# Six blocks of an MLP's second product by Strassen's algorithm, on one core

## Chip, cores and metric

The kernel runs on one core of a Trainium2 chip. The metric is the device time of one execution in microseconds (us).

## What is computed

The reference is a trunk of two layers over 512 tokens of 1024 channels, in float32. Each layer is a token mixer and an MLP with a hidden width of 4096. A conditioning vector `c` gives each of the four sub-layers a shift, a scale and a gate (`ada_mod`, one product of `c` with a matrix of 1024 by 3072):

```python
m = (jax.nn.silu(c) @ w + b)[:, None, :]
shift, scale, gate = jnp.split(m, 3, axis=-1)
...
u = x * (1.0 + scale) + shift
y = jnp.square(jax.nn.relu(u @ mlp_w1[layer] + mlp_b1[layer])) @ mlp_w2[layer] + mlp_b2[layer]
x = layer_norm(ALPHA * x + (1.0 + gate) * y, ln_g[layer, 1], ln_b[layer, 1])
```

The change is in the second MLP (`mlp(1, ...)`, the last piece of the program), in its product with `mlp_w2`, and in where the gate of that MLP is worked out.

## The kernel before

Every large product is made of three matmuls: each float32 operand is split into a rounded high part and a low part, and high × high, high × low and low × high are added up in PSUM. ScalarE (ACT) writes the high part by a cast, VectorE (DVE) the low part by a subtraction. For weights the parts are `wh` and `wl`, made from a staged slab `ws` of 1 MB (two buffers); for the hidden activations they are `hh` and `hl`, made from `r`, the output of the ReLU.

An MLP (`mlp`, L1043) cuts its hidden width into 8 blocks of 512. `up(b)` (L1048) makes one block of hidden channels for all 512 tokens: 4 slices × 8 pieces of the depth × 3 = 96 matmuls of 128 x 512. `down(b)` (L1080) multiplies that block with 512 rows of `mlp_w2` and adds into `Y`, held as 4 token tiles × 2 halves of 512 columns: 4 × 2 × 4 × 3 = 96 matmuls. The order is up(0), then up(1), down(0), up(2), down(1), to down(7).

Weights come by a list, `self.wlist` (`plan_weights`, L311): `w_dma` (L356) loads the next slab on the queue of SyncE (SP), `w_pre` (L394) splits it, `w_take` hands it to the product. A load waits until the split of the slab two places earlier is done.

The shifts, scales and gates are made piece by piece while an MLP runs. `ada_steps` (L209) is a generator: one step loads two tiles `ast` of a matrix, scales them and adds them into `acc`; four steps finish one job of 512 columns; after that two `pada` matmuls with a matrix of ones sum `acc` over its partitions (`finish`, L232). One of two generators does its additions on POOL (GpSimd), with the scaling on ACT, the other on DVE. `tick()` (L290) moves both by one step. The loops of `up` and `down` call it twice each, so 28 times in the first MLP; `self.tick(99)` behind the loop, ahead of down(7), runs what is left. The first MLP's list has six jobs (L1508). The gate of the last MLP, the jobs (3, 4) and (3, 5), is started in the last MLP:

```python
            if b == 1 and last:
                self.ada = [self.ada_steps([(3, 4)], "g", True), self.ada_steps([(3, 5)], "v", True)]
```

When a job is done and another follows, `acc` is split into `acch` and `accl`, and its sum is two matmuls of 512 columns; the last job's sum is one fp32 matmul.

In the last MLP POOL also works on the residual rows (`residuals`, L559, called by `step`): 16 additions or products of 128 x 512 (`X`) and 4 scalings (`rA`, `rB`).

Calls to the engines go through a helper, so the profile gives nearly all of them line L50; tiles are told apart by name. A scheduler fixes each engine's order when the program is built, and each engine and each DMA queue works its list in order.

Of the kernel before, what the change touches and what calls it, by code (L numbers as in the profile page):

```python
# [18 lines left out]
P = 128  # L19
# [17 lines left out]
PRED = mybir.dt.uint32  # L37

# [35 lines left out]
class Trunk:  # L74
# [26 lines left out]
    def setup(self):  # L101
# [29 lines left out]
        self.gate_d = {2: self.dram.tile([1, D], F32, name="gated2")}  # L131
# [77 lines left out]
    def ada_steps(self, jobs, eng, halved):  # L209
# [22 lines left out]
        def finish(n, cb, *acc):  # L232
            pt = self.ps("pada")
            for q, a in enumerate(acc):
                nc.tensor.matmul(pt, self.ones if len(acc) == 1 else self.ones_r, a,
                                 start=(q == 0), stop=(q == len(acc) - 1))
            if cb < 4:
                row = self.s2(f"mrow{n}_{cb}")[0:1, :]
                nc.scalar.copy(row, pt[0:1, :])
                nc.sync.dma_start(self.mod_d[n][:, cb * 512:cb * 512 + 512], row)  # L240
            else:
                h = cb - 4
                if n == 2:
# [7 lines left out]
                if n == 2:  # L251
                    nc.sync.dma_start(self.gate_d[n][:, h * 512:h * 512 + 512], g)
# [58 lines left out]
    def plan_weights(self):  # L311
# [5 lines left out]

        def out(w, n):
# [4 lines left out]
        def mlp(l):  # L323
            w1, w2 = i["mlp_w1"][l], i["mlp_w2"][l]
            up = lambda b: [("ch", w1, b * 512, 256), ("ch", w1, b * 512 + 256, 256)]
            dn = lambda b: [("rows", w2, b * 512, 2 * l + 1), ("rows", w2, b * 512 + 256, 2 * l + 1)]
            L.extend(up(0))
# [3 lines left out]

        self.wsmall = set()

        def alternate(n0):
            for q in range(n0, len(L)):
                if (q - n0) // 2 % 2:
                    self.wsmall.add(q)

        n0 = len(L)
        out(i["ev_w_out"][0], 0)  # L340
        mlp(0)
        alternate(n0)
# [7 lines left out]
        out(i["od_w_out"][0], 2)  # L350
        mlp(1)
        alternate(n0)
# [3 lines left out]
    def w_dma(self):  # L356
        d = self.wlist[self.n_dma]
        kind, w = d[0], d[1]
        if kind == "ch":
# [34 lines left out]
    def w_pre(self, eng=None):  # L394
# [8 lines left out]
        kind = d[0]  # L403
        small = self.n_split in self.wsmall
# [18 lines left out]
        self.n_split += 1  # L423

# [618 lines left out]
    def mlp(self, l, X, rest, last):  # L1043
# [4 lines left out]
        def up(b):  # L1048
            hh, hl = self.u8("hh"), self.u8("hl")
            ws = self.w_take() + self.w_take()  # L1050
# [10 lines left out]
            for f in range(4):  # L1061
                if b == 0:
# [3 lines left out]
                if f % 2 == 0:  # L1066
                    self.w_pre()
                col = 64 + l * 32 + b * 4 + f
                r, h2 = self.s2("r"), self.s2("h2")
# [8 lines left out]
            return hh, hl  # L1078

# [424 lines left out]
    def run(self):  # L1504
# [3 lines left out]
        self.ada = [self.ada_steps([(1, 4), (2, 0), (2, 2), (2, 4), (3, 0), (3, 2)], "g", True),  # L1508
                    self.ada_steps([(1, 5), (2, 1), (2, 3), (2, 5), (3, 1), (3, 3)], "v", True)]
# [32 lines left out]
```

## Time and profile before

| | |
|---|---|
| runs | 1270.35, 1271.13, 1271.96 us |
| median | 1271.13 us |
| profiled execution | 1276.4 us, of which the span is 1274.7 us |
| mean granted clock of TensorE | 0.988 of full speed |
| busy share of PE, DVE, ACT, POOL | 96%, 72%, 46%, 40% |
| read from HBM | 172.1 MB |

The profile is of one execution, with times from the start of its span. PE is TensorE's matmul side, PEld its weight loads, SPq the queue of loads and stores. A row of the timeline groups equal instructions in a row; a bracket at its end gives the idle time before it and what ended it. Matmuls overlap at their ends, so their pitch is read from their starts. In the profile the first MLP ends at about 600 us; the last one begins at 911 and runs to the end.

### The profile page before, as it was taken

To read this page: it belongs to the slowest core of one execution; us is meant where nothing else is said; L and a number is where in the kernel's file an instruction comes from. 1 tells how busy PE (TensorE), PEld (TensorE's weight loads), DVE (VectorE), ACT (ScalarE), POOL (GpSimd) and SP (SyncE) were. 2 spreads that over 40 slices of the span, in tenths; PEclk is the share of its full clock that TensorE was granted. 3 is DMA by queue.
4 is the path that set the end of the run, shared out by engine and by line. 5 is a ranking of instruction groups with operands and counts; after the bars stand their busy time and mean duration, and the time that the engine had idled before them with its cause. 6 is when DMAs were issued, how large, how long until landed. Compare 5 with 4: busy or idle time off the path is not lost. (4 is left out here: it accounts for less than half of the span.)

```text
span 1274.7 us, 17852 instructions
## 1 busy us (share of the span) xinstructions
PE 1226.4 (96%) x6529; PEld 1044.1 (82%) x6529; DVE 917.2 (72%) x1470; ACT 587.0 (46%) x1028; POOL 513.3 (40%) x524
## 2 busy tenths in 40 slices
PE   5899899999999999999999999999899999999997
PEld 4687678888888888888999999887888788888886
DVE  7879887867878766879578878778767745543656
ACT  2376553453544443523666677752453332322321
POOL 3466421538312320376256557558438000000166
PEclk9899999999999999999999999999899999999999
DMA  9757414262775456524232232343261624232311
GB/s 282 213 198 262 169 63 157 96 225 74 248 255 195 162 198 231 178 87 118 83 101 84 67 93 67 109 165 100 83 232 67 214 66 132 71 114 81 133 33 66
DMA packets 131529, 177.51 MB, mean 139 GB/s; under 512 B 9270, under 2 KB 87764, under 8 KB 131442
## 3 DMA queue, kind: packets, MB, share of 16 engines
q1 hardware_dynamic: 131330, 176.33, 43.0%
q8 instruction: 51, 0.84, 0.3%
q14 instruction: 36, 0.29, 0.1%
q10 hardware_dynamic: 112, 0.05, 0.0%
HBM read 172.10 MB, written 4.26 MB: 138 GB/s over the span
## 5 line engine op out<-in xcount | busy, mean ns | idle before, releaser
L50 DVE TENSOR_TENSOR wl<-ws,wh 128x512 fp32r<-128x512 f32 (+1 forms) x255 | 269.8, 1083 | 69.4 <-ACT wh L50 64.7
L50 ACT CAST wh<-ws 128x1024 fp32r<-128x1024 f32 (+2 forms) x271 | 207.7, 808 | 202.1 <-PE p L50 81.4
L50 PE MATMUL p<-uh,wh 128*128 128x512 f32 (+1 forms) x576 | 206.2, 366 | 0.0
L50 PE MATMUL p<-uh,wl 128*128 128x512 f32 (+1 forms) x576 | 205.9, 365 | 0.0
L50 PE MATMUL p<-wh,hh 128*128 128x512 f32 (+1 forms) x516 | 201.0, 390 | 0.0
L50 PE MATMUL p<-wh,hl 128*128 128x512 f32 (+1 forms) x516 | 200.0, 388 | 0.0
L50 PE MATMUL p<-wl,hh 128*128 128x512 f32 (+1 forms) x516 | 199.9, 387 | 0.0
L50 PE MATMUL p<-ul,wh 128*128 128x512 f32 (+1 forms) x576 | 192.9, 366 | 0.0
L50 POOL TENSOR_TENSOR acc<-acc,ast 128x512 f32<-128x512 f32 x70 | 102.8, 1468 | 205.1 <-ACT ast L50 111.7
L50 DVE TENSOR_TENSOR h<-r 128x512 f32<-128x512 f32 x64 | 52.7, 826 | 125.9 <-ACT r L50 124.6
L50 PEld LDWEIGHTS p<-uh,wl 128*128 128x128 f32 x576 | 108.7, 189 | 17.6
L50 PEld LDWEIGHTS p<-uh,wh 128*128 128x128 f32 x576 | 108.6, 189 | 17.4
L50 PEld LDWEIGHTS p<-ul,wh 128*128 128x128 f32 x576 | 100.9, 189 | 17.3
L50 PEld LDWEIGHTS p<-wl,hh 128*128 128x128 f32 x516 | 96.9, 188 | 20.2 <-issue 0.5
L50 PEld LDWEIGHTS p<-wh,hh 128*128 128x128 f32 x516 | 96.9, 188 | 20.0 <-ACT hh L50 0.2
L50 PEld LDWEIGHTS p<-wh,hl 128*128 128x128 f32 x516 | 96.9, 188 | 19.9
L50 ACT ACTIVATE r<-p,colA 128x512 f32<-128x512 f32 x64 | 43.8, 685 | 148.4 <-PE p L50 148.1
L50 POOL TENSOR_TENSOR ws<-ws,gate 128x512 f32<-128x512 f32 x16 | 25.0, 1596 | 210.9 <-DMA ws<-in_mlp_w_dram 210.9
L50 DVE TENSOR_TENSOR Y<-Y,p 128x512 f32<-128x512 f32 x96 | 64.7, 680 | 41.0 <-PE p L50 40.3
L50 DVE SCALAR_TENSOR_TENSOR acc<-ast,cs,acc 128x512 f32<-128x512 f32 x70 | 83.8, 1198 | 14.2 <-DMA ast<-in_ada_w_dram 13.8
L50 ACT ACTIVATE ast<-ast,cs 128x512 f32<-128x512 f32 x70 | 49.8, 721 | 93.2 <-DMA ast<-in_ada_w_dram 91.1
L50 POOL TENSOR_TENSOR ul<-u,uh 128x512 fp32r<-128x512 f32 x32 | 44.5, 1403 | 82.8 <-ACT uh L50 70.0
(317 smaller groups left out, 2686.2 us busy)
## 6 DMA issues: line engine op xcount, KB each, us to landing
ws<-in_mlp_w_dram SPq DMA_DIRECT2D x64, 1024.0 KB
ast<-in_ada_w_dram SPq DMA_DIRECT2D x160, 256.0 KB
ws<-in_od_w_in_dram SPq DMA_DIRECT2D x16, 1024.0 KB
ast<-in_ada_w_dram SPq DMA_DIRECT2D x16, 512.0 KB
ws<-in_ev_w_in_dram SPq DMA_DIRECT2D x7, 1024.0 KB
ws<-in_ev_w_out_dram SPq DMA_DIRECT2D x4, 1024.0 KB
nf<-fd SPq DMA_DIRECT2D x16, 256.0 KB
ws<-in_od_w_out_dram SPq DMA_DIRECT2D x4, 1024.0 KB
```

What stands on the lines that cost most here:

```text
L50: x = f(*a, **k)
```

## The change

The last MLP works in three groups of two hidden blocks, then two blocks as before. In a group, `up(g, True)` and `up(g + 1, True)` keep the hidden block unsplit (`hr`, float32). The product of 512 tokens × 1024 hidden × 1024 columns is then taken as a 2 × 2 product of blocks of 256 tokens × 512 hidden and 512 hidden × 512 columns, in Winograd's form of Strassen's algorithm: seven block products, each of 2 × 4 × 3 = 24 matmuls. `factor` forms the sums of hidden blocks (S1 to S4) in place in `hr` and splits them into high and low parts (`ha`, or `hah` and `hal`); `wino_b` does the same for the weights (T1 to T4, in `ws` and in four tiles `wE`), which `wino_dma` loads; B22 is loaded twice. The results stay in PSUM where two products share a sum, or go to `U2`, `Q7`, `Q5`, `C11`, `D21`, `D12` in SBUF, which are put together after the third group.

The gate of the last MLP moves: its jobs (3, 4) and (3, 5) are the seventh of the first MLP's lists, and its row goes through DRAM (`gated`, like that of the sub-layer before) and is read back ahead of up(6).

```diff
+WINOGRAD = (1,)
+WINO_B = ("B11", "T3", "T1", "T2", "B21", "T4", "B22")
+WINO_A = ("A11", "S3", "S1", "S2", "A12", "A22", "S4")
+WINO_SRC = {"B11": (0, 0), "T3": (0, 1), "B21": (1, 0), "B22": (1, 1)}
...
-                if n == 2:
+                if n >= 2:
                     g = self.s2(f"grow{n}_{h}")[0:1, :]
...
+            if l in WINOGRAD:
+                for g in range(0, 6, 2):
+                    L.extend(up(g) + up(g + 1) + [("wino", w2, g * 512, x) for x in WINO_B])
+                L.extend(up(6) + up(7) + dn(6) + dn(7))
+                for b in (n0 + 2, len(L) - 6, len(L) - 2):
+                    self.wsmall |= {b, b + 1}
+                return
...
+    def wino_dma(self, w, r0, which):
+        nc = self.nc
+        block = lambda r, c: w[r:r + 512, c:c + 512].rearrange("(k p) f -> p k f", p=P)
+        st = None
+        if which in WINO_SRC:
+            r, c = WINO_SRC[which]
+            st = self.wp.tile([P, 4, 512], F32, tag="ws", bufs=WS_BUFS, name="ws")
+            nc.sync.dma_start(st, block(r0 + 512 * r, 512 * c))
+        if which == "T3":
+            E = [self.s2(f"wE{k}") for k in range(4)]
+            for k in range(4):
+                nc.sync.dma_start(E[k], w[r0 + 512 + k * P:r0 + 512 + k * P + P, 512:1024])
+            self.wE_next = E
+        self.wstage[self.n_dma] = st
+        self.n_dma += 1
+    def wino_b(self, which, st):
+        nc = self.nc
+        sub = lambda o, a, b: nc.vector.tensor_tensor(o, a, b, op=ALU.subtract)
+        r = []
+        def halves(src, a):
+            hi, lo = [self.wp.tile([P, 2, 512], F32R, tag=x, name=x) for x in ("wh", "wl")]
+            if isinstance(src, list):
+                for j in range(2):
+                    nc.scalar.copy(hi[:, j], src[a + j])
+                    sub(lo[:, j], src[a + j], hi[:, j].bitcast(F32))
+            else:
+                nc.scalar.copy(hi, src[:, a:a + 2, :])
+                sub(lo, src[:, a:a + 2, :], hi.bitcast(F32))
+            return [(hi[:, j], lo[:, j]) for j in range(2)]
+        if which == "B11":
+            self.wB11 = st
+        elif which == "T3":
+            self.wE, self.wB12 = self.wE_next, st
+            for k in range(4):
+                sub(self.wE[k], self.wE[k], st[:, k])
+        if which == "T1":
+            for a in (0, 2):
+                x = self.wB12[:, a:a + 2, :]
+                sub(x, x, self.wB11[:, a:a + 2, :])
+                r += halves(self.wB12, a)
+            for k in range(4):
+                nc.vector.tensor_tensor(self.wE[k], self.wE[k], self.wB11[:, k], op=ALU.add)
+            return r
+        for a in (0, 2):
+            r += halves(self.wE if which in ("T3", "T2", "T4") else st, a)
+        if which == "B21":
+            for k in range(4):
+                sub(self.wE[k], st[:, k], self.wE[k])
+        return r
...
-        def up(b):
+        def up(b, raw=False):
+            if raw:
+                hh, hl = self.u8("hr", F32), None
+            else:
+                hh, hl = self.u8("hh"), self.u8("hl")
+            ws = self.w_take() + (self.w_take() if b == 0 or not raw else [])
...
                 nc.scalar.activation(hh[:, f], r, AF.Square)
-                nc.vector.tensor_tensor(h2, r, r, op=ALU.mult)
-                nc.vector.tensor_tensor(hl[:, f], h2, hh[:, f].bitcast(F32), op=ALU.subtract)
+                if not raw:
+                    h2 = self.s2("h2")
+                    nc.vector.tensor_tensor(h2, r, r, op=ALU.mult)
+                    nc.vector.tensor_tensor(hl[:, f], h2, hh[:, f].bitcast(F32), op=ALU.subtract)
...
+        def factor(name, H, q):
+            a = [H[0][:, :, 0:256], H[0][:, :, 256:512]] + ([H[1][:, :, 0:256], H[1][:, :, 256:512]] if H[1] else [])
+            sub = lambda o, x, y: nc.vector.tensor_tensor(o, x, y, op=ALU.subtract)
+            if q % 3 < 2:
+                t = self.u8("ha", F32R, (2, 4, 256))
+                parts = [(slice(0, 4), t[:, 0], t[:, 1])]
+            else:
+                parts = [(slice(f, f + 2), *[self.s2(x, F32R).rearrange("p (k t) -> p k t", k=2) for x in ("hah", "hal")])
+                         for f in (0, 2)]
+            if name == "S3":
+                sub(a[1], a[0], a[1])
+            elif name == "S1":
+                sub(a[1], a[3], a[1])
+                nc.vector.tensor_tensor(a[0], a[0], a[1], op=ALU.add)
+            elif name == "S4":
+                sub(a[2], a[2], a[1])
+            src = a[{"A11": 0, "S3": 1, "S1": 0, "S2": 1, "A12": 2, "A22": 3, "S4": 2}[name]]
+            terms = []
+            for fs, hi, lo in parts:
+                nc.scalar.copy(hi, src[:, fs])
+                sub(lo, src[:, fs], hi.bitcast(F32))
+                terms += [(hi[:, k], lo[:, k]) for k in range(fs.stop - fs.start)]
+            return terms
+        def winograd(g, acc, H, first):
+            ops = list(first)
+            pts = {}
+            plan = [("1", False, "U2", None), ("7", False, "Q7", None), ("5", False, "Q5", 1), ("6", False, "U2", None),
+                    ("1", True, "C11", 0), ("7", True, "D21", 0), ("5", True, "D12", 1)]
+            for q, (bank, on, to, bias) in enumerate(plan):
+                if len(ops) < min(q + 3, 7):
+                    ops.append(factor(WINO_A[len(ops)], H, len(ops)))
+                w = self.w_take()
+                self.w_pre()
+                if not on:
+                    pts[bank] = [self.ps("p2") for _ in range(2)]
+                for k in range(4):
+                    for t in range(2):
+                        tok = slice(t * P, t * P + P)
+                        lh, ll = [x[:, tok] for x in ops[q][k]]
+                        for n3, (x, y) in enumerate(((lh, w[k][0]), (lh, w[k][1]), (ll, w[k][0]))):
+                            nc.tensor.matmul(pts[bank][t], x, y, start=(not on and k == 0 and n3 == 0),
+                                             stop=(k == 3 and n3 == 2), skip_group_check=True)
+                ops[q] = None
+                for t in range(2):
+                    if (to, t) in acc:
+                        nc.vector.tensor_tensor(acc[to, t], acc[to, t], pts[bank][t], op=ALU.add)
+                        continue
+                    acc[to, t] = self.s2(f"{to}{t}")
+                    if bias is None:
+                        nc.vector.tensor_copy(acc[to, t], pts[bank][t])
+                    else:
+                        nc.vector.tensor_tensor(acc[to, t], b2[bias], pts[bank][t], op=ALU.add)
...
-        Y = [[self.s2(f"Y{t}_{h}") for h in range(2)] for t in range(NT)]
-        prev = up(0)
-        for b in range(1, nb):
-            if b == 1 and last:
-                self.ada = [self.ada_steps([(3, 4)], "g", True), self.ada_steps([(3, 5)], "v", True)]
-            cur = up(b)
-            down(b - 1, *prev)
+        if l in WINOGRAD:
+            acc = {}
+            for g in range(0, 6, 2):
+                H = [up(g, True)[0], None]
+                first = [factor(WINO_A[q], H, q) for q in range(2)]
+                H[1] = up(g + 1, True)[0]
+                winograd(g, acc, H, first)
+            for t in range(2):
+                for x, y in (("D12", "U2"), ("D21", "U2"), ("Q7", "Q5"), ("Q7", "U2")):
+                    nc.vector.tensor_tensor(acc[x, t], acc[x, t], acc[y, t], op=ALU.add)
+            Y = [[acc["C11", t], acc["D12", t]] for t in range(2)] + [[acc["D21", t], acc["Q7", t]] for t in range(2)]
+            del acc
+            self.gates[n] = self.bc(self.gate_d[n], f"gate{n}")
+            prev = up(6)
+            cur = up(7)
...
-        self.ada = [self.ada_steps([(1, 4), (2, 0), (2, 2), (2, 4), (3, 0), (3, 2)], "g", True),
-                    self.ada_steps([(1, 5), (2, 1), (2, 3), (2, 5), (3, 1), (3, 3)], "v", True)]
+        self.ada = [self.ada_steps([(1, 4), (2, 0), (2, 2), (2, 4), (3, 0), (3, 2), (3, 4)], "g", True),
+                    self.ada_steps([(1, 5), (2, 1), (2, 3), (2, 5), (3, 1), (3, 3), (3, 5)], "v", True)]
```

On PE the end of the first MLP changes. `p2_5228` is the last product of down(6), `p2_5317` the first of down(7), `pmod` a transposition of the next shift and scale. Before, the fp32 sums stood ahead of down(6):

```order
L50 MATMUL p1_4894<-uh1_2142,wl_4830 128x512
L50 MATMUL pada_5041<-acc3_2_4682,ones_81 128x512
L50 MATMUL pada_5046<-acc3_3_4690,ones_81 128x512
L50 MATMUL p2_5051<-wh_4921,hh_4518 128x512
L50 MATMUL p2_5051<-wl_4922,hh_4518 128x512
```

Now:

```order
L55 MATMUL p2_5228<-wh_5010,hl_4520 128x512
L55 MATMUL pada_5263<-acch_5159,ones_r_83 128x512
L55 MATMUL pada_5263<-accl_5160,ones_r_83 128x512
L55 MATMUL pada_5277<-acch_5169,ones_r_83 128x512
L55 MATMUL pada_5277<-accl_5170,ones_r_83 128x512
L55 MATMUL pada_5295<-acc3_4_5054,ones_81 128x512
L55 MATMUL pada_5300<-acc3_5_5062,ones_81 128x512
L55 MATMUL pmod_5307<-ident_76,modr2_5305 128x16
L55 MATMUL p2_5317<-wh_5095,hh_4890 128x512
```

The sums of (3, 2) and (3, 3) went from two fp32 matmuls ahead of down(6) to four of the split kind behind it, and those of (3, 4) and (3, 5) stand between them and `pmod`.

On SP, at the same place, the loads of the last two pieces of `ast` and the store of the gate are new. Before, the three slabs of `od_w_in` followed `modr`:

```order
L50 DMA modd_110<-mrow_2_5043 1x512
L50 DMA modd_110<-mrow_3_5048 1x512
L50 DMA ws<-in_od_w_in_dram 128x8x256
L50 DMA modr_5223<-modd_109 16x128
L50 DMA ws<-in_od_w_in_dram 128x8x256 x3
```

Now:

```order
L55 DMA ws<-in_od_w_in_dram 128x8x256 x2
L55 DMA ast_5_3_0_5273<-in_ada_w_dram 128x512
L55 DMA ast_5_3_1_5275<-in_ada_w_dram 128x512
L55 DMA gb_0_5285<-in_ada_b_dram 128x512
L55 DMA modd_110<-mrow_2_5266 1x512
L55 DMA modd_110<-mrow_3_5280 1x512
L55 DMA gb_1_5291<-in_ada_b_dram 128x512
L55 DMA ws<-in_od_w_in_dram 128x8x256
L55 DMA gated_112<-grow_0_5297 1x512
L55 DMA modr_5305<-modd_109 16x128
```

`ast_5_3` and `modr` are now behind the third slab and `modr` behind a store that waits for the gate.

On DVE, in the last MLP's first group, from the end of up(0) on, before (`h` and `hl` are the square and its low part):

```order
L50 TENSOR_TENSOR hl<-h_9902,hh 128x512
L50 TENSOR_TENSOR h_9954<-r 128x512
L50 TENSOR_TENSOR hl<-h_9954,hh 128x512
L50 TENSOR_TENSOR h_9988<-r 128x512
L50 TENSOR_TENSOR hl<-h_9988,hh 128x512
L50 TENSOR_SCALAR acc_5_10009<-ast_5_0_0_9915,cs 128x512
```

Now:

```order
L55 TENSOR_TENSOR wl<-wE_9892,wh 128x512
L55 TENSOR_TENSOR wl<-wE_9893,wh 128x512
L55 TENSOR_TENSOR wE_9890<-wE_9890,ws 128x512
L55 TENSOR_TENSOR wE_9891<-wE_9891,ws 128x512
L55 TENSOR_TENSOR wE_9892<-wE_9892,ws 128x512
L55 TENSOR_TENSOR wE_9893<-wE_9893,ws 128x512
L55 TENSOR_TENSOR hr<-hr 128x4x256 x2
L55 TENSOR_TENSOR wl<-ws,wh 128x1024
L55 TENSOR_TENSOR hal<-hr,hah 128x512 x2
L55 COPY U_10108<-p_10082 128x512
L55 COPY U_10110<-p_10083 128x512
```

The squares' low parts are gone from here, and block sums of weights (`wE`) and of hidden blocks (`hr`), with their low parts, stand in their place.

## Rows read from the trace of the kernel before

**Rows 1.** The page, busy time (share of the span) and instructions of each engine.
```profile
PE 1226.4 (96%) x6529; PEld 1044.1 (82%) x6529; DVE 917.2 (72%) x1470; ACT 587.0 (46%) x1028; POOL 513.3 (40%) x524
```

**Rows 2.** Windows: stretch, its length, busy us (instructions) of five engines, PE clock, DMA.
```profile
core 0: us, PE busy (x) PEld busy (x) DVE busy (x) ACT busy (x) POOL busy (x), PEclk, DMA share, GB/s
550.00:575.00 25.00, 25.00 (x108) 20.02 (x107) 15.78 (x19) 7.89 (x14) 16.45 (x13) 1.00 0.30 85
950.00:975.00 25.00, 25.00 (x112) 20.71 (x111) 18.40 (x13) 7.58 (x13) 24.75 (x18) 1.00 0.20 72
1000.00:1025.00 25.00, 23.14 (x97) 17.88 (x97) 18.72 (x27) 10.33 (x18) 1.93 (x2) 1.00 0.39 135
1025.00:1050.00 25.00, 25.00 (x112) 20.68 (x112) 9.59 (x13) 7.63 (x12) 0.00 (x0) 1.00 0.27 85
```

**Rows 3.** The chain that ended last, in order of time: start, us, what.
```profile
992.57 6.20 DMA ast<-in_ada_w_dram
...
1003.88 1.12 PE pada L50 x2
1005.00 255.72 PE p L50 x1128
```

**Rows 4.** Timeline of PE, end of the first MLP: start, us, instruction.
```profile
554.49 1.88 PE L50 MATMUL pada<-acc,ones 128*128 128x512 f32 x4
555.80 0.79 PE L50 MATMUL p<-wh,hh 128*128 128x512 f32 x1
...
578.10 0.23 PE L50 MATMUL pmod<-ident,modr 16*128 16x16 f32 x1
```

**Rows 5.** Timeline of the SP queue, end of the first MLP.
```profile
528.11 0.33 SPq L50 DMA_DIRECT2D ast<-in_ada_w_dram  x1
...
565.93 18.04 SPq L50 DMA_DIRECT2D ws<-in_od_w_in_dram  x3
```

**Rows 6.** Timeline of DVE, end of the first MLP.
```profile
563.02 2.88 DVE L50 TENSOR_TENSOR wl<-ws,wh 128x512 fp32r<-128x512 f32 x2
...
575.22 3.88 DVE L50 TENSOR_TENSOR wl<-ws,wh 128x1024 fp32r<-128x1024 f32 x2 [1.76 <-ACT wh L50]
```

**Rows 7.** Timeline of ACT, before down(6) of the first MLP.
```profile
530.80 0.72 ACT L50 ACTIVATE ast<-ast,cs 128x512 f32<-128x512 f32 x1 [1.11 <-DMA ast<-in_ada_w_dram]
```

**Rows 8.** Timeline of POOL, end of the first MLP, first and last row of eleven.
```profile
561.98 3.37 POOL L50 TENSOR_TENSOR Y<-Y,gate 128x512 f32<-128x512 f32 x2 [8.55 <-DVE Y L50]
...
586.04 1.29 POOL L50 TENSOR_TENSOR X<-X,Y 128x512 f32<-128x512 f32 x1
```

**Rows 9.** Timeline of POOL, last MLP, first and last row of the residual work.
```profile
945.81 0.62 POOL L50 TENSOR_SCALAR rA<-rA 128x512 f32<-128x512 f32 x1 [19.40 <-DMA rA<-in_ln_g_dram]
...
960.59 13.37 POOL L50 TENSOR_TENSOR X<-X,rB 128x512 f32<-128x512 f32 x8
```

**Rows 10.** Timeline of DVE, last MLP, beside that work and after it.
```profile
964.24 3.47 DVE L50 TENSOR_TENSOR wl<-ws,wh 128x512 fp32r<-128x512 f32 x2
...
974.44 2.47 DVE L50 TENSOR_TENSOR Y<-b,p 128x512 f32<-128x512 f32 x4
...
986.67 0.74 DVE L50 SCALAR_TENSOR_TENSOR acc<-ast,cs,acc 128x512 f32<-128x512 f32 x1
```

**Rows 11.** Timeline of PE, last MLP, the end of up(1) and the start of down(0).
```profile
956.98 0.39 PE L50 MATMUL p<-uh,wl 128*128 128x512 f32 x1
957.20 0.39 PE L50 MATMUL p<-wh,hh 128*128 128x512 f32 x1
```

**Rows 12.** Groups of DVE's instructions by shape, 1040 to 1205: busy, mean ns | idle before.
```profile
L50 DVE TENSOR_TENSOR wl<-ws,wh 128x512 fp32r<-128x512 f32 x32 | 20.3, 685 | 0.0
L50 DVE TENSOR_TENSOR wl<-ws,wh 128x1024 fp32r<-128x1024 f32 x16 | 19.5, 1222 | 7.6 <-ACT wh L50 7.0
```

**Rows 13.** Timeline of PE after a gap, ahead of the last MLP.
```profile
898.05 1.97 PE L50 MATMUL pt<-ident,X 128*128 128x128 f32 x8 [3.35 <-DVE X L50]
...
901.52 0.63 PE L50 MATMUL pw<-wl,mh 128*128 128x512 f32 x1
901.95 0.63 PE L50 MATMUL pw<-wh,ml 128*128 128x512 f32 x1
```

More of the change, by code (lines that the diff above doesn't have):

```diff
@@ L130, in setup @@
         self.mod_d = {n: self.dram.tile([1, 2 * D], F32, name=f"modd{n}") for n in range(1, 4)}
-        self.gate_d = {2: self.dram.tile([1, D], F32, name="gated2")}
+        self.gate_d = {n: self.dram.tile([1, D], F32, name=f"gated{n}") for n in (2, 3)}
     def ada_bias(self):
@@ L250, in finish @@
                 nc.vector.scalar_tensor_tensor(g, pt, 1.0, bias, op0=ALU.add, op1=ALU.add)
-                if n == 2:
+                if n >= 2:
                     nc.sync.dma_start(self.gate_d[n][:, h * 512:h * 512 + 512], g)
@@ L316, in plan_weights, with alternate @@
               ("ch", win, 2048, 256), ("ch", win, 2304, 256), ("ch", win, 640, 128), ("ch", win, 768, 256)]
+        self.wsmall = set()
+        def alternate(n0):
+            for q in range(n0, len(L)):
+                if (q - n0) // 2 % 2:
+                    self.wsmall.add(q)
         def out(w, n):
@@ L330, in mlp @@
             L.extend(dn(7))
[L332 to L337, printed above, removed]
+            alternate(n0)
         n0 = len(L)
         out(i["ev_w_out"][0], 0)
+        alternate(n0)
         mlp(0)
-        alternate(n0)
         win = i["od_w_in"][0]
@@ L350, in plan_weights @@
         out(i["od_w_out"][0], 2)
+        alternate(n0)
         mlp(1)
-        alternate(n0)
         self.wlist, self.n_dma, self.n_split, self.n_take = L, 0, 0, 0
@@ L358, in w_dma @@
         kind, w = d[0], d[1]
+        if kind == "wino":
+            return self.wino_dma(*d[1:])
         if kind == "ch":
@@ L403, in w_pre @@
         kind = d[0]
+        if kind == "wino":
+            self.wready[self.n_split] = self.wino_b(d[3], st)
+            self.n_split += 1
+            return
         small = self.n_split in self.wsmall
@@ L1061, in up @@
             for f in range(4):
+                if f == 2 and len(ws) < 4:
+                    ws = ws + self.w_take()
+                if f % 2 == 0 and b and raw:
+                    self.w_pre()
                 if b == 0:
@@ L1065, in up @@
                     self.proj_ch(pts[f], ws[f])
-                if f % 2 == 0:
+                if f % 2 == 0 and not (b and raw):
                     self.w_pre()
                 col = 64 + l * 32 + b * 4 + f
-                r, h2 = self.s2("r"), self.s2("h2")
+                r = self.s2("r")
                 nc.scalar.activation(r, pts[f], AF.Relu, bias=self.colA[:, col:col + 1])
                 nc.scalar.activation(hh[:, f], r, AF.Square)
-                nc.vector.tensor_tensor(h2, r, r, op=ALU.mult)
-                nc.vector.tensor_tensor(hl[:, f], h2, hh[:, f].bitcast(F32), op=ALU.subtract)
+                if not raw:
+                    h2 = self.s2("h2")
+                    nc.vector.tensor_tensor(h2, r, r, op=ALU.mult)
+                    nc.vector.tensor_tensor(hl[:, f], h2, hh[:, f].bitcast(F32), op=ALU.subtract)
                 if b:
@@ L1123, in mlp @@
         b2 = self.bc(i["mlp_b2"][l:l + 1, :], f"b2{l}")
-        Y = [[self.s2(f"Y{t}_{h}") for h in range(2)] for t in range(NT)]
-        prev = up(0)
-        for b in range(1, nb):
-            if b == 1 and last:
-                self.ada = [self.ada_steps([(3, 4)], "g", True), self.ada_steps([(3, 5)], "v", True)]
-            cur = up(b)
-            down(b - 1, *prev)
-            prev = cur
+        if l in WINOGRAD:
[13 more added lines that the diff above has]
+            cur = up(7)
+            down(6, *prev)
+            prev = cur
+        else:
+            Y = [[self.s2(f"Y{t}_{h}") for h in range(2)] for t in range(NT)]
+            prev = up(0)
+            for b in range(1, nb):
+                cur = up(b)
+                down(b - 1, *prev)
+                prev = cur
         self.tick(99)
```

4 lines of the change are left out of this document (2 added, 2 removed).

## The prediction

> **What bounds the kernel now.** The busy shares come first [rows 1]: TensorE (PE) is busy for 96% of the span, VectorE (DVE) for 72%. The table by stretches says where the last MLP differs from that mean [rows 2]: from 1025 on PE fills all 25 us of a stretch and DVE has 9.6; from 950 to 975 DVE has 18.4 and GpSimd (POOL) 24.8; from 1000 to 1025 PE loses time, 97 matmuls instead of 112. The chain that ended last [rows 3] says the same: 1128 matmuls in a row, 255.72 us, behind one pause in which a load of the conditioning weights (`ast`) landed 6.20 us after its issue and two column sums (`pada`) followed. So the last MLP is bound by PE, at 255.72 / 1128 = 0.2267 us per 512-column matmul, and every matmul taken out there is worth that, as long as its operands are ready. The other thing to see is that PE's queue is in order: a matmul that waits for a sum holds up all that stand behind it.
>
> **Removed matmuls.** Two blocks of the second product cost 192 matmuls before and 7 × 24 = 168 now; three groups save 72. 72 × 0.2267 = **−16.3 us**.
>
> **Conditioning work moved out of the last MLP.** The pause of 1000 to 1025 goes, with its two `pada`: 15 matmuls' time, 15 × 0.2267 = **−3.4 us**. Nothing else is late there, since PE waits for nothing on either side of it [rows 3].
>
> **The same work put at the end of the first MLP.** The loop of the first MLP has 28 ticks. Six jobs take 24 pieces and two steps around them, 26; seven take 30, so the last piece and the two fp32 sums of the jobs (3,4) and (3,5) now come in the flush behind the loop. The order shows it: before, `pada` stands ahead of down(6), at 554.49, and then PE runs on to `pmod` at 578.10 [rows 4]; now six `pada` stand between down(6) and `pmod`, and down(7), ready or not, is behind them. PE gets there at 578.1 − 1.3 (the four records at 554.49, gone) + 0.9 (four halves) = 577.7. The sums need the last two pieces of `ast`, and their loads stand on the SP queue behind the third `od_w_in` slab, which needs the slot that DVE frees with its second 1024-column split. I go along that chain:
> - The two splits began at 575.22 and took 3.88, so the second ended at 579.1 before [rows 6]. Ahead of it DVE now has eight more 512-column operations (six `acc`, two `accl`), at 0.74 alone or 3.47 / 2 = 1.74 beside POOL [rows 10]: 5.9 to 13.9 us, against 25 − 15.8 = 9.2 us of idle time [rows 2]. That delays the split by 0 to 4.7; I take the middle, 581.5, because POOL worked from 561.98 to 587.3 without a gap [rows 8] and has seven more additions.
> - Two more issues at 0.33 [rows 5] and 6.20 to land behind a slab [rows 3]: 588.4. Two `acc` operations of 1.74: 591.9. The pair of `pada`, 1.12 [rows 3]: 593.0.
> - `pmod` waits too: its load `modr` stands on SP behind the store of the gate's first half. 0.74 for that row on DVE and 2.7 for a load on an empty queue (issued 528.11, used 530.80 [rows 5, 7]): 596.4.
>
> That is 596.4 − 578.1 = **+18 us**. The low end takes the split at its old time, a load of 2.7 and lone DVE prices: 579.1 + 0.7 + 2.7 + 1.5 + 1.1 + 3.4 = 588.5, +10. The high end takes the split at 583.8 and a microsecond for the stores, +22. The middle is nearest to the rows, since slab and POOL are both there. Whatever follows on PE, up to the last MLP, comes later by as much. An idle PE also starts slowly: after the 3.35 us gap at 898 it ran at half its granted clock, matmuls 0.43 apart (901.52, 901.95) [rows 13]; eight of those cost 8 × 0.2 = 1.6. With the second short wait for `pmod` I take **+2 us**.
>
> **DVE in the first group.** POOL's twenty operations on the residual rows run from 945.8 to 974 [rows 9] whatever the group does, as the loads that release them keep their place. Beside them a DVE operation with both inputs in SBUF took 1.74 for 512 columns and 3.88 / 2 = 1.94 for 1024; alone the pitch is 0.6 and 1.14 (0.69 and 1.22 recorded, less the overlap) [rows 6, 10, 12]; one that reads PSUM stayed at 0.62, four `Y` in 2.47 [rows 10]. Before, the stretch held few such operations; now it holds the block sums. Once POOL starts, nine operations of 512 and two of 1024 (rest of T3, T1, T2 and T3's low half) stand ahead of S2: 9 × 1.74 + 2 × 1.94 = 19.5, so until 965.3 instead of 953.5. S2's inputs are there about 1.3 after up(1) ends at 957.2 [rows 11], so the delay is 965.3 − 958.5 = 6.8. Then S2 and S1's sums, one split and two `hal`: 3 × 1.94 + 2 × 1.74 = 9.3 instead of 4.6. So S1, the operand of the third product, is ready at 958.5 + 6.8 + 9.3 + 3.5 = 978, where PE wants it at 957.2 + 2 × 24 × 0.2267 = 968.1: 10 us. With the mildest row, 2.88 / 2 = 1.44 for 512 columns [rows 6], the same sum gives 974.8 and 7 us. The low halves of an operand come one by one and PE can begin with the first, so I take **+8 us**; the low end is half of the mild case, 3, and the high one 10 and 2 for the backlog that DVE carries on, 12.
>
> The Trainium skill, on the page "SBUF — State Buffer", section "Who interferes with whom", has it that a DVE instruction with two SBUF inputs and a GpSimd one that reads SBUF exclude each other for a whole instruction. By it a 1024-column operation should cost 1.14 + 1.29 = 2.4 beside POOL, where the row shows 1.94; seven of them would add 3 us to this place and make the total 1283. The measurement decides, so the sum keeps 1.94.
>
> **DVE in the other groups.** POOL is idle from 1025 on [rows 2]. Seven products last 168 × 0.2267 = 38.1 us on PE; DVE's list for them holds 12 operations of 1024 and 27 of 512, 12 × 1.14 + 27 × 0.6 = 29.9. It fits, with a wait at the third product where S1 comes just in time: **+1 us** for both groups, ends 0 (all hidden) and 5 (DVE a quarter slower).
>
> **Costed at nothing.** The 68 more ACT instructions: ACT is busy for 7.6 of 25 us [rows 2], and PE waits for ACT only if that doubles. The 3 MB of second reads of B22: the DMA share is 0.20 to 0.39 there [rows 2]; if it were full, a slab would come some microseconds late. The gate through DRAM: used 100 us later.
>
> **Sum.** −16.3 − 3.4 + 18 + 2 + 8 + 1 = +9.3 us. The profiled execution took 1276.4, so 1285.7 by its clock; the median of the runs, 1271.13, is 5.3 lower, and the forecast is 1271.1 + 9.3 = **1280.4 us**.
>
> **Rivals.**
> 1. *The covers hold: faster.* One mechanism decides at both places, the price of a DVE operation beside POOL. If the schedules interleave so that most cost 0.74, the first MLP's stall falls to its low end (10 + 1.6) and the first group's to 3: −19.7 + 11.6 + 3 = −5, **1266 us**. It turns at stalls of 19.7 in all. For it: from 945.8 to 954 POOL and DVE hardly met. Against it: the rows of 964 to 974, one after the other at 1.74. 0.20.
> 2. *Nothing stalls.* The sums reach `pada` by 577.7, and only the matmuls count: −19.7 + 1 = **1252 us**. Against it: the slot is not free before 579.1 even in the old order. 0.04.
> 3. *DVE becomes the bound of all three groups.* Operations on strided halves of `hr` (256 of 512 columns) have no row here; at a third more for all, 29.9 becomes 39.9 against 38.1, and with the sums at the group's start some 5 us a group are lost: **1291 us**. Against it: nothing in the rows makes them slower. 0.12.
>
> **Chances and range.** The forecast has 0.64, with a range of its own of 1271 to 1291 from the ends above. No difference under 0.2% (2.5 us) can be told from none: faster 0.22 (rivals 1 and 2, less their slow edge), same 0.08, slower 0.70. The range of 1262 to 1293 takes in rivals 1 and 3 and leaves out 2.
>
> **What would show it.** The step is right if PE has a gap of over 8 us between the four halves and the fp32 `pada` near 577, released by `acc`, and a second one at `pmod`; if the stretch of 965 to 990 later in the trace (shifted by the first stall) loses PE time to DVE's `ha`, `hal` or `wl`; if DVE's operations there take 1.7; and if the last two groups run without a gap. It is wrong if PE goes from down(6) to down(7) in under 4 us, or if gaps of several microseconds stand in every group.

## The result, and the profile after

The changed kernel took 1284.51 us (median of five) against 1271.13 before: ratio 1.0101, 95% interval 1.008 to 1.0122. One of the five took 2019.18 us at a mean granted clock of 0.558 and is left out of the ratio; the other four lie at 1282.07 to 1287.72, at clocks of 0.980 to 0.985. The change is slower by about 13 us. The profiled execution took 1282.07 us, its span 1280.3.

The busy line of the page shows that the removed matmuls are gone (6457 for 6529 in [rows 1]), with 12 us of PE time, and that DVE has 72 us more:

```profile
PE 1214.2 (95%) x6457; PEld 1030.8 (81%) x6457; DVE 989.1 (77%) x1523; ACT 627.4 (49%) x1073; POOL 520.8 (41%) x524
```

So PE works less and the kernel is longer: PE must stand still more. The windows after (columns as in [rows 2]) show where:

```profile
575.00:600.00 25.00, 8.89 (x18) 4.77 (x19) 17.98 (x20) 2.95 (x4) 21.21 (x13) 0.59 0.55 168
950.00:975.00 25.00, 25.00 (x125) 21.24 (x124) 22.04 (x21) 14.20 (x22) 12.10 (x9) 1.00 0.34 124
975.00:1000.00 25.00, 20.92 (x86) 15.45 (x84) 24.96 (x18) 11.80 (x17) 22.33 (x12) 1.00 0.25 84
1000.00:1025.00 25.00, 23.21 (x100) 18.60 (x101) 22.38 (x30) 8.62 (x11) 0.00 (x0) 1.00 0.36 112
1025.00:1250.00 225.00, 225.00 (x994) 186.38 (x993) 158.69 (x193) 103.86 (x143) 28.66 (x20) 1.00 0.36 117
```

Two places lose time that the kernel before does not lose there: the end of the first MLP, where PE is busy for 8.89 of 25 us, and the first group of the last MLP, 975 to 1025. From 1025 on, where the other two groups lie, PE is busy for 225 of 225 us.

**The end of the first MLP.** The timeline of PE, which answers to [rows 4]:

```profile
574.17 0.39 PE L55 MATMUL pada<-accl,ones_r 128*128 128x512 f32 x1
587.05 2.08 PE L55 MATMUL pada<-acc,ones 128*128 128x512 f32 x2 [12.50 <-POOL acc L55]
592.70 2.08 PE L55 MATMUL pada<-acc,ones 128*128 128x512 f32 x2 [3.57 <-DVE acc L55]
595.26 0.28 PE L55 MATMUL pmod<-ident,modr 16*128 16x16 f32 x1 [0.48 <-DMA modr<-modd]
595.47 0.80 PE L55 MATMUL p<-wh,hh 128*128 128x512 f32 x1
596.07 0.63 PE L55 MATMUL p<-wl,hh 128*128 128x512 f32 x1
596.50 0.63 PE L55 MATMUL p<-wh,hl 128*128 128x512 f32 x1
...
599.53 0.39 PE L55 MATMUL p<-wl,hh 128*128 128x512 f32 x1
```

Behind the four halves PE waits 12.50 us for the sum of POOL, 3.57 for that of DVE and 0.48 for the load `modr`; then its matmuls start 0.43 us apart up to 599 and 0.23 after that, so it runs at half the clock till then. On the SP queue ([rows 5] before) the last two `ast` and `modr` stand where the order had them:

```profile
576.84 6.01 SPq L55 DMA_DIRECT2D ws<-in_od_w_in_dram  x2
582.95 1.00 SPq L55 DMA_DIRECT2D ast<-in_ada_w_dram  x2
...
593.27 0.24 SPq L55 DMA_DIRECT2D gated<-grow  x1
593.60 0.32 SPq L55 DMA_DIRECT2D modr<-modd  x1
```

and on DVE ([rows 6]) the split that frees the slot, then the two `acc` behind the loads:

```profile
577.93 4.51 DVE L55 TENSOR_TENSOR wl<-ws,wh 128x1024 fp32r<-128x1024 f32 x2
...
589.23 3.41 DVE L55 SCALAR_TENSOR_TENSOR acc<-ast,cs,acc 128x512 f32<-128x512 f32 x2 [1.15 <-DMA ast<-in_ada_w_dram]
```

**The first group.** The waits of PE from 950 to 1250 (line waited for, us in total, times, longest) are all behind DVE's low halves:

```profile
PE p L55 <- DVE wl L55: 4.6, 6, 1.3
PE p L55 <- DVE hal L55: 1.2, 1, 1.2
```

The one for the hidden block, and the last of those for weights, on PE:

```profile
988.29 0.50 PE L55 MATMUL p<-wh,hal 128*128 128x512 f32 x1 [1.20 <-DVE hal L55]
...
1008.48 0.50 PE L55 MATMUL p<-wl,ha 128*128 128x512 f32 x1 [0.60 <-DVE wl L55]
```

DVE is there beside POOL's residual work, which ends at 997.3 ([rows 9, 10] before):

```profile
970.93 2.79 DVE L55 TENSOR_TENSOR wl<-wE,wh 128x512 fp32r<-128x512 f32 x2
973.65 6.20 DVE L55 TENSOR_TENSOR wE<-wE,ws 128x512 f32<-128x512 f32 x4
979.77 4.54 DVE L55 TENSOR_TENSOR hr<-hr 128x1024 f32<-128x1024 f32 x2
984.24 2.31 DVE L55 TENSOR_TENSOR wl<-ws,wh 128x1024 fp32r<-128x1024 f32 x1
986.47 3.46 DVE L55 TENSOR_TENSOR hal<-hr,hah 128x512 fp32r<-128x512 f32 x2
...
991.06 1.21 DVE L55 TENSOR_TENSOR wl<-ws,wh 128x1024 fp32r<-128x1024 f32 x1
...
1007.21 1.22 DVE L55 TENSOR_TENSOR wl<-ws,wh 128x1024 fp32r<-128x1024 f32 x1
```
```profile
980.96 16.37 POOL L55 TENSOR_TENSOR X<-X,rB 128x512 f32<-128x512 f32 x8
```

A 1024-column operation takes 2.27 to 2.31 us beside POOL and 1.22 once POOL is done; one `wl`, behind two copies out of PSUM, took 1.21 beside POOL all the same. POOL's eight take 2.05 each on average. The waits come to 5.8 us; with the slower starts behind each of them, the matmuls of this group start 8.1 us later in all than at their usual 0.2267. The chain that ended last agrees: it goes through DVE's `wE`, `hr`, `wl` and `hal` up to a last piece on PE that is now this long ([rows 3] before, 1128 matmuls):

```profile
1007.29 1.15 DVE wl L55
1008.48 257.81 PE p L55 x1136
```

### The profile page after: what moved, and what is told of

Its sections match the earlier page's. It is cut to its first block, busy times and chain, and to the rows that moved or that the text cites. A ratio compares the mean times of both kernels' runs of the same rounds, so it can differ in the third digit from the quotient of the medians.

```text
span 1280.3 us, 17812 instructions
## 1 busy us (share of the span) xinstructions
PE 1214.2 (95%) x6457; PEld 1030.8 (81%) x6457; DVE 989.1 (77%) x1523; ACT 627.4 (49%) x1073; POOL 520.8 (41%) x524
## 5 line engine op out<-in xcount | busy, mean ns | idle before, releaser
L55 DVE TENSOR_TENSOR wl<-ws,wh 128x1024 fp32r<-128x1024 f32 (+1 forms) x235 | 269.2, 1165 | 89.6 <-ACT wh L55 86.9
L55 PE MATMUL p<-wh,hh 128*128 128x512 f32 (+1 forms) x324 | 126.3, 390 | 0.0
L55 PE MATMUL p<-wl,hh 128*128 128x512 f32 (+1 forms) x324 | 125.9, 388 | 0.0
L55 PE MATMUL p<-wh,hl 128*128 128x512 f32 (+1 forms) x324 | 125.8, 388 | 0.0
L55 DVE TENSOR_TENSOR h<-r 128x512 f32<-128x512 f32 x40 | 36.2, 908 | 53.1 <-ACT r L55 53.1
L55 PE MATMUL p<-wh,ha 128*128 128x512 f32 x240 | 75.1, 389 | 0.0
L55 PE MATMUL pqk<-wh,uh 128*128 128x256 f32 x256 | 74.1, 290 | 0.0
L55 PE MATMUL pqk<-wh,ul 128*128 128x256 f32 x256 | 72.5, 284 | 0.0
L55 PE MATMUL pqk<-wl,uh 128*128 128x256 f32 x256 | 72.4, 283 | 0.0
```

Source lines behind the costliest of these rows:

```text
L55: x = f(*a, **k)
```

## The experiments

**Theory.** Two separate stalls undo the saving. At the end of the first MLP the sums of the added job hold PE's in-order queue; in the first group POOL's residual work slows DVE. **Rivals.** The block sums alone are too much for DVE; or other things at these places are late anyway, so that taking a holder away frees nothing.

All traces are cut at the same points, so that stages can be compared: A from the first layer's last `pmod` (near 218) to the one ahead of the last MLP (near 885 to 905), which holds the first MLP and the mixer; B the last MLP, from its first to its last product; C what follows. The ratio goes with its interval.

| kernel | ratio to before | A us | B us | C us |
|---|---|---|---|---|
| before | | 667.5 | 355.6 | 8.4 |
| the change | 1.0101 [1.008, 1.0122] | 688.2 | 343.4 | 8.4 |
| e5 no Strassen, gate moved | 1.0172 [1.0148, 1.0195] | 687.3 | 351.5 | 8.3 |
| e1 residual late | 1.0061 [1.0038, 1.0083] | 687.5 | 335.2 | 14.0 |
| e3 ticks earlier | 1.004 [1.0023, 1.0057] | 684.6 | 343.6 | 8.8 |
| e4 both | 1.0002 [0.9986, 1.0017] | 684.1 | 335.3 | 14.0 |
| e7 ticks spread, residual late | 1.0036 [1.002, 1.0053] | 687.7 | 335.2 | 14.0 |
| e6 flush behind down(7) | 1.0058 [1.0037, 1.0078] | 685.4 | 344.0 | 8.8 |
| e8 e6, residual late | 1.0038 [1.0024, 1.0053] | 685.4 | 335.3 | 12.6 |
| e11 e6, `modr` early | 1.003 [1.0018, 1.0041] | 679.9 | 343.7 | 8.8 |
| e12 e11, residual in up(2), up(4) | 0.9974 [0.996, 0.9988] | 682.1 | 337.3 | 8.5 |
| e9 gate and residual late | 0.9923 [0.99, 0.9946] | 666.9 | 340.5 | 12.8 |
| e10 gate late, residual as e12 | 0.9922 [0.9909, 0.9936] | 667.3 | 345.1 | 8.3 |
| e13 e10, gate behind the groups | 0.992 [0.9906, 0.9933] | 670.1 | 339.5 | 11.6 |

Stages with the same code differ by 1 to 3 us between executions (A of e11 and e12), and the stretch ahead of A, which no edit touches, took 214.3 to 218.6 us. So a stage shows a stall of 4 us and more; less needs the ratio.

**e5: the move of the gate alone.**

```diff
-WINOGRAD = (1,)
+WINOGRAD = ()
...
+            if last:
+                self.gates[n] = self.bc(self.gate_d[n], f"gate{n}")
```

> The change without its Strassen products: the last MLP's second product is in the old form, the gate of that MLP is still made in the first MLP. Theory (the moved conditioning work costs its own stall, and PE's in-order queue carries it to the end): the gap of 12.5 + 3.6 us ahead of pmod stays, pmod about 20 us later than before, 2 us of half clock after it, and the pause of 3.4 us in the last MLP goes, so 20 + 2 - 3.4 = 18 to 19 us slower than before, ratio 1.014 to 1.015. Rival (the stall is given back later, or the loss is that of the block products): within 3 us of before, ratio 0.998 to 1.003.

Ratio 1.0172, so about 22 us slower than before, a little above what was expected. Its waits at the end of the first MLP are those of the change, 12.5, 3.6 and 0.5 us; B is 355.6 − 351.5 = 4.1 shorter without the gate's pause and its sums. The move of the gate alone makes the kernel slower, by more than Strassen's form, with the stall of its first group, gives back.

**e1: the residual work later.** The steps are kept for up(6) and up(7).

```diff
-                    self.step(2)
+                    if l == 0 or b >= 6:
+                        self.step(2)
```

> The changed kernel with POOL's work on the residual rows done in up(6) and up(7) and not in up(1). Theory (DVE beside POOL is what makes the first group late): the seven waits of PE on wl and hal there, 5.8 us, and the lost matmuls go to under 1.5 us, DVE's operations of 1024 columns there fall from 2.3 to 1.2 us, and the kernel is 5 to 7 us faster than the changed one, ratio to before about 1.005. Rival (the chain of slab loads at the group's start, 5.09 and 4.99 us on the chain that ended last, sets it): DVE's operations are fast, but PE still loses 4 to 6 us between up(1) and the fourth product, ratio 1.009 to 1.011.

PE waits for nothing between 930 and 1250, and B falls to 335.2: the 8 us of the first group were POOL's, and with POOL away DVE keeps up with all three groups. This excludes the rival that the block sums alone are too much, and the one in the expectation that the slab loads at the group's start set the pace. But C grows by 5.6. In e4, with the same edit, POOL works without a pause through down(6) and up to 1261, since the residual rows' work now meets its share of down(6), and the chain that ended last has 6.23 us of "issue" on DVE at 1255.5, with no releaser shown; that this is POOL's backlog is inferred, not shown. Windows of before, then of e4 (columns as in [rows 2]):

```profile
1225.00:1250.00 25.00, 25.00 (x112) 20.72 (x111) 14.04 (x19) 3.18 (x7) 21.73 (x16) 1.00 0.00 1
```
```profile
1225.00:1250.00 25.00, 25.00 (x112) 20.71 (x111) 17.93 (x27) 4.72 (x9) 25.00 (x19) 1.00 0.00 0
```

**e3 and e4: the jobs of the first MLP earlier.** Four more ticks in up(1) and up(2), so that the flush finds nothing left; e4 has e1's edit too.

```diff
-                    if f % 2:
+                    if f % 2 or (l == 0 and b < 3):
```

> The changed kernel with four more ticks in the first MLP (blocks 1 and 2 of up call one per slice), so that the seven jobs end in up(7) as the six did and no fp32 sum stands between down(6) and down(7). Theory: the gap ahead of pmod goes whole, 19.8 us and 1.7 us of half clock: 20 to 22 us faster than the changed kernel, ratio to before about 0.993 to 0.995. Rival (the gap comes from DVE and POOL having too much to do at the end of the first MLP, wherever the sums stand): pmod is late by 8 us or more all the same, ratio 1.000 to 1.005.

> Both edits together: residual rows late and four more ticks. If the two stalls are all that the change costs, only the 72 matmuls and the moved pause are left, -16.3 - 3.4 + 1 = -19 us, 1252 us, ratio 0.985. If DVE binds the block products in each group, or the residual work collides anew in up(6) and up(7), ratio 0.990 or more.

Both missed. The wait ahead of `pmod` is gone, and one of the same size stands at the first sum of that MLP (PE of e3):

```profile
334.40 1.32 PE L55 MATMUL pada<-acch,ones_r 128*128 128x512 f32 x2 [11.49 <-ACT acch L55]
```

`acch` waits for POOL's `acc`, and that for its `ast`, which are loaded between the slabs of `mlp_w1`. The windows of before, then of e3, show the DMA engines busy for 0.92 of the stretch, so they have little to give there:

```profile
325.00:350.00 25.00, 25.00 (x112) 20.72 (x111) 20.26 (x21) 14.48 (x25) 10.19 (x7) 1.00 0.73 254
```
```profile
325.00:350.00 25.00, 15.60 (x60) 12.63 (x61) 20.35 (x24) 13.53 (x21) 11.03 (x7) 0.80 0.92 310
```

The added job was pushed from one in-order wait into another.

**e7: the four ticks spread over up(3) to up(6).** With e1's edit.

```diff
-                    if f % 2:
+                    if f % 2 or (l == 0 and 3 <= b < 7 and f == 0):
```

> Residual rows late, and the four more ticks in blocks 3 to 6 of the first MLP, one each, where the run with ticks in blocks 1 and 2 had them pulled into its start and lost 11 us at the first sum. Theory: no gap at the first sum, none ahead of pmod, none in the first group: -16.3 - 3.4 + 1 = -19 us, 1252 to 1254 us, ratio 0.985 to 0.987. Rival (the seven jobs do not fit the first MLP anywhere, since DVE and POOL are the limit there): some gaps of PE of 8 us or more in all between 350 and 580, ratio 0.992 or more.

Missed again: four waits of 1.3 to 4.1 us at the sums of three jobs, 12.4 in all, and the restarts at half the clock; A stays at 687.7. One, on PE:

```profile
388.89 0.50 PE L55 MATMUL pada<-accl,ones_r 128*128 128x512 f32 x1 [3.90 <-DVE accl L55]
```

**e6 and e8: the flush behind down(7).** PE then meets the late sums only when down(7) is done; e8 has e1's edit too.

```diff
-        self.tick(99)
         if last:
+            self.tick(99)
...
         down(nb - 1, *prev, mid=mid, after=after, byhalf=True)
+        self.tick(99)
```

> The changed kernel with one line moved: the flush of the conditioning steps stands behind down(7) of the first MLP, so on PE the two fp32 sums come after down(7). All work and all loads are the same. Theory (the in-order queue holds down(7) behind sums that are late): pmod follows the four halves within 1 us, the sums are ready when down(7) ends 22 us later, and the kernel is 17 to 21 us faster than the changed one, ratio to before 0.994 to 0.997. Rival (DVE and POOL have too much to do there, and whatever PE does next waits for them): a gap of 8 us or more opens at the residual sums behind down(7), ratio 1.002 to 1.006.

> The moved flush and the late residual rows. Theory: both stalls gone without more ticks, -16.3 - 3.4 + 1 and up to 3 for what is left around the flush, ratio 0.985 to 0.989. Rival as for the moved flush alone, then 0.994 or more.

Both missed: A fell by 2.8 us only. `pmod` has become the one that waits (PE, then SP of e6):

```profile
591.21 0.26 PE L55 MATMUL pmod<-ident,modr 16*128 16x16 f32 x1 [15.58 <-DMA modr<-modd]
```
```profile
577.91 6.00 SPq L55 DMA_DIRECT2D ws<-in_od_w_in_dram  x2
584.01 1.01 SPq L55 DMA_DIRECT2D ast<-in_ada_w_dram  x2
585.11 0.64 SPq L55 DMA_DIRECT2D modr<-modd  x1
```

`modr`, 8 KB, stands behind two slabs and two tiles; it is issued at 585.11 and there at 591. So two queues held `pmod` at once, and freeing PE's alone is worth little.

**e11: `modr` early as well.** Its data has been in DRAM for long by then, so the load can stand ahead of down(6).

```diff
+                if b == nb - 1 and not last:
+                    self.mod_load(n + 1)
                 down(b - 1, *prev)
...
-        self.mod_load(n + 1)
```

> The flush of the last sums behind down(7), as in e6, and the load of modr put on the SP queue ahead of the ast tiles and slabs of that place (its data is stored some 100 us earlier). If two queues held pmod, PE's by the sums and SP's by the load: now neither does, pmod starts within 1 us of the four halves, the 15.6 us gap of e6 is gone and the ratio falls from 1.0058 to 0.990 to 0.994 (the first group's 8 us stay). Rival, something else ahead of pmod or of down(7) is late (the second slab, DVE's splits, the sum of Y): a gap of over 4 us stays within 10 us of pmod, ratio 1.000 or more.

Half right. `pmod` now follows the halves at 575.39 with no wait, so the two queues were the holders there. But the ratio is 1.003: 25 us later PE waits for the next thing (PE, then DVE of e11):

```profile
600.65 1.73 PE L55 MATMUL pt<-ident,X 128*128 128x128 f32 x7 [9.66 <-DVE X L55]
```
```profile
580.00 4.58 DVE L55 TENSOR_TENSOR wl<-ws,wh 128x1024 fp32r<-128x1024 f32 x2
...
588.75 1.57 DVE L55 TENSOR_TENSOR wl<-ws,wh 128x1024 fp32r<-128x1024 f32 x1
...
592.70 0.67 DVE L55 TENSOR_TENSOR X<-X,p 128x512 f32<-128x512 f32 x1
```

Before, DVE began that `X` at 584.67, 52.9 us behind the first half of the fifth sum; here it is 592.70 − 529.92 = 62.8 behind it. DVE has hardly a pause from 560 to 598. The list now holds two more `accl` (1.7 us each) and six more `acc` (0.74 to 1.67), some 10 us in all, and others, beside POOL, take longer than before. That these additions put the whole list back by 10 us is argued from the list; that the moved gate does it follows from e9 and e10 below. Of the change's 20.7 us in A, e11 gives back 8; the other 12 stay, and this list is the largest part of them.

**e12: e11 with the residual steps, one a slice, in up(2) and up(4).**

```diff
-                    self.step(2)
+                    if l == 0:
+                        self.step(2)
+                    elif b in (2, 4):
+                        self.step()
```

> e11 with the residual rows' POOL work one slice at a time in up(2) and up(4). Both stalls should be gone and nothing put in their place: last MLP 335 us, tail 8.7, pmod as in e11: -16.2 - 4.1 = -20.3 us, ratio 0.983 to 0.986. Rival, as for e10, that the collision only moves to the next groups: 0.990 or more.

B is 337.3 with one wait of 1.61 us left (on `hal`, in the second group), and C is as before. So POOL's work can go beside the second group for 2 us; why it costs less there than beside the first was not tested. The steps did not spread, though: POOL did all of them in one piece, from 1015.96 to 1047.5. The ratio missed by A's 14 us, as e11 had shown at the same time.

**e9, e10, e13: the gate back in the last MLP.** e9 starts its jobs ahead of up(4) and has e1's edit; e10 starts them ahead of up(2), and e13 at the end of up(5), both with e12's steps. Common to them:

```diff
-        self.ada = [self.ada_steps([(1, 4), (2, 0), (2, 2), (2, 4), (3, 0), (3, 2), (3, 4)], "g", True),
+        self.ada = [self.ada_steps([(1, 4), (2, 0), (2, 2), (2, 4), (3, 0), (3, 2)], "g", True),
...
             for g in range(0, 6, 2):
+                if g == 4:
+                    self.ada = [self.ada_steps([(3, 4)], "g", True), self.ada_steps([(3, 5)], "v", True)]
```

(`if g == 2` in e10). The ticks of the last MLP are in up(2), up(4), up(6) in e10, and in e13 at

```diff
-                    if f % 2:
+                    if (b, f) in ((5, 3), (6, 1), (6, 3), (7, 0), (7, 2), (7, 3)) if l else f % 2:
```

> Residual rows late, and the conditioning work of the gate back in the last MLP, started ahead of up(4), so that the first MLP is as before the change. Theory: nothing is left of the first stall; the sums come in up(6), where DVE and POOL have had 60 us for them: the 16.3 us of the matmuls less 1 to 3 for two sums and for DVE in the third group, ratio 0.987 to 0.990. Rival (DVE is full in the third group, and its eight additions stall the products): PE loses 4 us or more between up(5) and up(6), ratio 0.991 to 0.994.

> The seven products kept; the gate of the last MLP is made there again (started ahead of up(2), ticked only in up(2), up(4), up(6)), and the residual rows are scaled on POOL one slice at a time in up(2) and up(4). If the stall of the first group is POOL's work beside DVE, and the late tail of e9 came from putting that work at the very end: no gap of over 1.5 us in the first group, the last MLP 335.0 + 1.9 (two column sums) = 337 us long, the tail behind the last product at 8.7 as before and not 14.2, the first MLP as before: ratio 0.985 to 0.988. Rival, DVE beside POOL costs as much in the second and third group as in the first: gaps of 4 us or more in up(2) to up(5) and a ratio of 0.990 or more.

> As e10, but the gate's additions start at the end of up(5) and run in up(6) and up(7), behind the three groups, where DVE has slack. If e10 lost its time to the gate's additions standing among the group's block sums (DVE 25 of 25 us busy there, additions of 1.67 to 1.78 us beside POOL), that loss goes and only the two column sums stay: from the second pmod to the last product 358.85 (e12) + 1.9 = 361 us against 380.3 before, the first MLP as before, the tail 8.5: -19 us, ratio 0.984 to 0.987. Rival, the last sums wait for their ast tiles behind the slabs of up(7) and down(6), or for POOL: a gap of over 3 us ahead of pada and a ratio of 0.988 or more.

A is back to 667 in e9 and e10 (670 in e13, with no new wait): this stall came from the moved gate alone. All three are faster than both kernels, by about 10 us than the one before and by some 23 than the changed one. None reaches the 18 that the parts promised, and all three ratios lie outside what was expected: by the table each pays some 8 us at another place. e9 pays at the end (C 12.8) and with a wait of 3.22 us on `hal`. e10 pays in the second group, where the gate's additions stand among the block sums (PE of e10, then its windows):

```profile
1041.53 0.80 PE L55 MATMUL p<-wl,ha 128*128 128x512 f32 x1 [3.50 <-DVE wl L55]
```
```profile
1025.00:1050.00 25.00, 21.50 (x88) 17.35 (x87) 25.00 (x22) 9.64 (x14) 14.10 (x8) 0.93 0.05 12
1050.00:1075.00 25.00, 23.13 (x100) 18.33 (x99) 25.00 (x35) 13.73 (x19) 0.00 (x0) 1.00 0.34 116
```

DVE is busy for 50 of 50 us. e13 keeps B at 339.5, as expected (one wait of 1.64 us, and two column sums), but C grew by 3.2. The first half of the gate is there only at 1206.17; POOL, which multiplies by it for down(6), starts at 1206.25, which is 43 us ahead of the end of the last product where it was 61 before. From then on it is behind, busy for 25.00 of 25 us from 1225 to 1250, and the chain that ended last runs through it there (DVE, then the chain):

```profile
1205.49 0.68 DVE L55 SCALAR_TENSOR_TENSOR gate<-pada,gb 128x512 f32<-128x512 f32 x1
```
```profile
1234.04 1.25 POOL D L55
1235.29 1.25 POOL X L55
1236.54 1.25 POOL Q L55
```

The rest of its 8 us, 2.6 in A and 2.4 in B (1.64 of it that one wait), is of the size by which stages differ from one execution to the next.

## Why the prediction was right

The direction was right, and so were the places. The time, 1284.51, is 4 us above the forecast of 1280.4 and inside its own range. (That range, 1271 to 1291, is narrower than the ends it is drawn from: all low ends together give 1266, all high ones 1292.) Some of the closeness is luck, as the steps show:

- **−16.3 for the matmuls.** Between e5 and e4 B falls by 351.5 − 335.3 = 16.2.
- **−3.4 for the pause of the gate.** 4.1 (before against e5). The 97 matmuls that were set against 112 hold the four records of the two `pada`, so the pause and its sums cost 19 matmuls' time, 4.3, and not 15.
- **+18 and +2 at the end of the first MLP.** A grew by 20.7. The first half of the fifth sum is at 531.79 before and at 529.01 after; counted from there, `pmod` came 46.3 us later before and 66.3 after, 19.9 more, and the restart at half the clock 8 × 0.2 = 1.6 more. Within the chain three steps were off, and they nearly cancel, which is luck. The slot was freed 6.1 us later (582.4 − 529.0 against 579.1 − 531.8), where the forecast took 2.4 and at most 4.7: DVE had no idle time at all from 565 to 582. The pair of `pada` took 2.08 where 1.12 stood. `modr` cost less: PE waited 0.48 us for it behind the last sum, where 3.4 stood; the row's store had gone out at 593.27, while that sum ran, and PE had `modr` 1.66 us after its issue (593.60 to 595.26). The load of the two `ast` and the two `acc` came as forecast (582.95 to 589.23, and 3.41).
- **+8 in the first group.** 343.4 − 335.2 (e1) = 8.2. The size is right and the place only in part. The forecast had the third product 10 us late for its operand S1. In that working the last 3.5 has no row; it is what two `hal` cost, and two are in the 9.3 already. In the trace the third product starts on time, at 985.88 (48 matmuls behind the end of up(1) at 975.00); S1 is whole at 989.93, 4 us late, and PE waits 1.20 for its low half. The other 4.6 us of waits are for low halves of weights, from 986 to 1008. POOL's twenty operations did not keep their length, as the forecast had it: 962.4 to 997.3, 34.9 us, where they took 28 before, so DVE slowed POOL too. The price that went into it was too low for 1024 columns (1.94 where 2.27 to 2.31 came) and too high for some operations of 512: `wE` took 1.55 and the `wl` of `wE` 1.4 to 1.7 on average where 1.74 stood, since those that met POOL's scalings (`rA`, `rB`) took 1.1 and only those beside its additions 1.78. By the rule weighed there (the Trainium skill, "SBUF — State Buffer", "Who interferes with whom": the two engines exclude each other for a whole instruction) the estimate for a 1024-column operation beside POOL was 1.14 + 1.29 = 2.4. The trace is nearer to the rule than to the row of before that the forecast kept.
- **+1 in the other groups.** 0: 225 of 225 us.
- **Costed at nothing.** ACT has 45 instructions more (1073 for 1028), not 68, and PE waits for none of them in the last MLP.

The sum of these parts in the traces is −16.2 − 4.1 + 20.7 + 8.2 = +8.6, as forecast (+9.3). The runs differ by 13.4. The profiled execution of before lies 5.3 us above its median and that of the change 2.4 below its own, and 3 us of this can be seen in code that is the same in both: the stretch ahead of A (218.6 against 217.1) and the one between A and B (24.6 against 23.2). What the rest is made of stays open.

Rival 3, DVE as the bound of all three groups, is excluded by the 225 us without a gap and by e1. Rival 1 would have needed most of DVE's operations at 0.74 beside POOL; in the first group none of 512 columns with both inputs in SBUF that began while POOL was at work took less than 1.09, and most took 1.77 or 1.78.

What the forecast did not see is the third holder. It named PE's queue and, for `pmod`, the SP queue; that DVE's list is 10 us late for `X` in any case, and so that freeing both queues saves only 8 of the 20 us, came out of e11 alone.

## What to carry to other kernels

A cheaper algorithm on the busiest engine pays only if its operands' extra work finds free time on the other engines, stretch by stretch; here the saving of 16 us was lost to one moved helper job (20 us where it had cost 4) and to one neighbour on POOL (8 us), neither of them part of the algorithm. A wait that one edit takes away should be followed to what is late next before anything is promised: here PE's queue, the SP queue and DVE's list were late by 20, 16 and 10 us one behind the other, and each showed only when the one ahead was gone. Put work that only has to be done some time (gates, residual rows) where the table by stretches shows both its engine and its neighbours free; e9, e10 and e13 had it at three places, each time with a bill of its own, and still beat both kernels.

## What the runs showed of the hardware

- DVE and POOL slowed each other: `hr` on DVE took 2.27 beside POOL and 1.22 alone, POOL's `X` 2.05 on average beside DVE's two-input operations and 1.25 to 1.3 away from them (e12: 3.80 for three).
- An 8 KB load took 1.66 us from issue to use with no other load under way and 6.1 us (e6: 585.11 to 591.21) right behind two slabs of 1 MB and two tiles.
- After the gaps of 12.50 and 3.57 us the granted clock was 0.59 on average from 575 to 600: a pair of fp32 `pada` took 2.08 us where before it took 1.12 [rows 3], and eight matmuls came at half the pace before the full one returned.
